# Softmax row sums of a pair of heads: one product on four column tiles, reciprocals spread by SBUF transfers

## The chip, the cores and the metric

The kernel runs on one core of a Trainium2 chip. The metric is the device time of one execution in microseconds (us), lower is better; the figure for a kernel is the median of several runs.

## What is computed

Two layers of a hybrid backbone over 1024 latent tokens and 256 context tokens, width 1024. Layer 0 mixes with a recurrence and a Fourier transform. Layer 1, where the change lies, is attention with 16 heads of 64 values, queries of 1024 tokens over keys and values of all 1280 tokens, followed by a gate, an output projection and a layer norm:

```python
def attend(q, k, v):
    s = jnp.einsum('bqhd,bkhd->bhqk', q, k, preferred_element_type=jnp.float32) * ATTN_SCALE
    p = jax.nn.softmax(s, axis=-1).astype(v.dtype)
    return jnp.einsum('bhqk,bkhd->bqhd', p, v)
...
    o_l = blocked_attention(q_l, k_all, v_all).reshape(b_, s_, MLA_WIDTH)
    y_lat = (o_l * jax.nn.silu(g_l)) @ w_out
```

All data are float32. A softmax needs, for each head and query, the sum of the exponentials over all 1280 keys, and its reciprocal.

## The kernel before

**Loops.** The attention stage walks over eight pairs of heads (`p`, 0 to 7); a pair over two halves of the queries (`hf`, 512 each); a half over ten key tiles of 128 keys (`kt`, called units here). The two heads of a pair, `a`, lie on two row groups of TensorE, so that their score products run side by side. `attend` issues a unit's ten score products into one of two score tiles in PSUM (`s`), the exponential on ScalarE into one of six tiles `p`, and on GpSimd the addition of `p` to the running sum `ra` (128 keys by 2 heads by 512 queries), one such addition per unit. `pv` multiplies the exponentials of a unit with the values into `st["o"]`, the one bank of the pool `o_ps`; units 3, 5, 7 and 9 run it for two earlier units, and the last two units (8 and 9) are left to `rest`, which runs in the next half.

**The ends of a half.** `finish` gives a table of what the next half (or the next pair's first half) runs after a given unit. `rest` (unit 1): the last two `pv`, then on VectorE the gate tile `sgt` times the result `po`. `rows` (unit 3): the row sums, two products of `ra` with a 128x64 tile of ones on two column tiles, so that each head's sums stand on 64 rows of PSUM, the same on each, and a ScalarE copy to `ri`. `piece` 0 to 3 (units 4 to 7): the reciprocals of `ri` on VectorE, 128 columns at a time. `last` (unit 8): on VectorE `sgt` times `ri`, both in SBUF, and the store to `o_dr`. A pair runs all of it twice.

**What runs between.** While pair `p` is attended, the next is prepared. `near` and `far` hold steps that are run after a unit's scores and at its end. In units 2 to 17 of a pair's twenty they are mostly `max_pass`, which finds the greatest score of each query for pair `p + 1`: per tile of 128 queries three steps (512, 512 and 256 keys), each with two heads. A step takes two tiles `mx` of the pool `m_ps` (line 827), which has three banks that go round, writes both with TensorE (line 977) and reduces each on VectorE (line 979). An even unit has one step of 512 keys, an odd unit one of 512 near and one of 256 far. Also in `far`: in even pairs the weights of the next four heads (`prep_quad`, with the loads of the rotary tables `rc` and `rs`), in odd pairs the values (`prep_v`, one more bank of `m_ps`). Units 18 and 19 have no steps of the pass but its end. In pairs 6 and 7 the output weights are loaded and split (`wo1_load`, `wo1_high`, `wo1_low`, lines 1033 to 1050): a load waits until GpSimd has split what was in its buffer.

**Order.** TensorE, VectorE, ScalarE and GpSimd run what is written, in that order (`manual_schedule`, line 998). All loads and stores of this stage are issued by SyncE, one queue, whose order is set when the program is built; an issue that waits holds back those behind it.

Of the kernel before, what the change touches and what calls it, by code (L numbers as in the profile page):

```python
# [13 lines left out]
F32 = mybir.dt.float32  # L14
F32R = mybir.dt.float32r
AF = mybir.ActivationFunctionType
ALU = mybir.AluOpType
# [4 lines left out]
P = 128  # L22
# [5 lines left out]
NT = T // P  # L28
# [26 lines left out]
def _body(ctx, tc, ap, out, dbg=None):  # L55
# [4 lines left out]
    def load(o, i):  # L60
        nc.sync.dma_start(out=o, in_=i)
# [801 lines left out]
    def prep_quad(q):  # L863
# [23 lines left out]
        def ra(hf):  # L887
            c = slice(512 * hf, 512 * hf + 512)

            def product():  # L890
                pa = m_ps.tile([P, 512], F32, tag="m", name=f"pra{q}{hf}")
                for k in range(2):
                    mm3(pa, wh[:, k, 2, :], wl[:, k, 2, :], qnh[k][:, c], qnl[k][:, c], k == 0, k == 1)
                rc = pr_p.tile([P, 512], F32, tag="rc", name=f"rc{q}{hf}")
                load(rc, ap["ropec_cm"][:, c])
                rs = pr_p.tile([P, 512], F32, tag="rs", name=f"rs{q}{hf}")
                load(rs, ap["ropes_cm"][:, c])
                rot = pr_p.tile([P, 512], F32, tag="rot", name=f"rot{q}{hf}")
                V.stream_shuffle(out=rot, in_=pa, mask=[i ^ 8 for i in range(32)])
                V.tensor_tensor(out=rc, in0=rc, in1=pa, op=ALU.mult)  # L900
                st[hf] = rc, rs, rot

            def turn():
                rc, rs, rot = st[hf]
                G.tensor_tensor(out=rot, in0=rot, in1=rs, op=ALU.mult)
                G.tensor_tensor(out=rot, in0=rot, in1=rc, op=ALU.add)

            def parts():
                split(roth[:, c], rotl[:, c], st[hf][2], S, G)

            return [product, turn, parts]
# [146 lines left out]
    def attend(p, hf, kt, st):  # L1058
# [2 lines left out]
        c = slice(512 * hf, 512 * hf + 512)  # L1061
        ks = slice(P * kt, P * kt + P)
        if kt == 0:
            st["sg"] = at.tile([P, 512], F32, tag="sgt", bufs=2, name=f"sgt{p}{hf}")
            load(st["sg"], sg_dr[p][:, c])
            st["o"] = o_ps.tile([P, 512], F32, tag="o", name=f"po{p}{hf}")
            st["ra"] = at.tile([P, 2, 512], F32, tag="ra", bufs=2, name=f"ra{p}{hf}")
            if p == 7:
                st["rv"] = at.tile([P, 2, 512], F32, tag="rv", name=f"rv{hf}")
            st["e"] = []  # L1070
        b = p % 2
        ps = s_ps.tile([P, 2, 512], F32, tag="s", name=f"s{p}{hf}{kt}")

# [17 lines left out]
    def pv(p, st, k):  # L1091
        q, i = divmod(p, 2)
        for a in range(2):
            TE.matmul(st["o"][64 * a : 64 * a + 64, :], quad[q][6][:, k, 128 * i + 64 * a : 128 * i + 64 * a + 64],  # L1094
                      st["e"][k][:, a, :], start=(k == 0), stop=(k == NT - 1), tile_position=(0, 64 * a))

    def finish(p, hf, st):

        c = slice(512 * hf, 512 * hf + 512)

        def rest():
            for k in (8, 9):
# [21 lines left out]
            load(o_dr[p][:, c], st["sg"])  # L1124

        if p == 7 and hf == 0:
            return {1: [rest], 2: [rows], 3: [piece(0), piece(1)], 4: [piece(2)], 5: [piece(3), last]}
        return {1: [rest], 3: [rows], 4: [piece(0)], 5: [piece(1)], 6: [piece(2)], 7: [piece(3)], 8: [last]}

    def o_load(t):  # L1130
# [16 lines left out]
    for p in range(8):  # L1147
# [37 lines left out]
        for hf in range(2):  # L1185
            st = {}
            for kt in range(NT):
                g = NT * hf + kt
                attend(p, hf, kt, st)
                for u in near[g]:  # L1190
                    u()
                if kt > 2 and kt % 2:
                    pv(p, st, kt - 3)
                    pv(p, st, kt - 2)
                for u in tail.get(kt, ()):
                    u()
                for u in far[g]:
                    u()
                if p == 7 and g == 18:
                    os_ = {0: o_load(0)}  # L1200
            tail = finish(p, hf, st)

    s_psc()
    f_ps, f_psc = pool("f_ps", 2, space=PSUM)
# [184 lines left out]
```

## Time and profile before

| what | value |
|---|---|
| median of three runs | 1445.64 us (1443.05 to 1446.84) |
| the profiled execution, its own time | 1445.85 us |
| its span, first to last instruction | 1444.0 us |
| TensorE busy | 1396.4 us (97%) |
| VectorE, GpSimd, ScalarE busy | 911.3, 678.7, 542.2 us |
| attention, from the first scores of pair 0 to the last of pair 7 | 838.1 to some 1340 us |

The profile is one execution on the chip. Times in its views are us from the span's start, PE is TensorE, DVE is VectorE, ACT is ScalarE, POOL is GpSimd, SPq is SyncE's queue. A float32 product shows as two matmul records. Matmul ends are modelled, so what a group of products costs is read from where the next one starts. A TensorE that waits in its queue can still look busy; the chain of waits and the starts tell it.

### The profile page before, as it was taken

To read this page: it belongs to the slowest core of one execution; us is meant where nothing else is said; L and a number is where in the kernel's file an instruction comes from. 1 tells how busy PE (TensorE), PEld (TensorE's weight loads), DVE (VectorE), ACT (ScalarE), POOL (GpSimd) and SP (SyncE) were. 2 spreads that over 40 slices of the span, in tenths; PEclk is the share of its full clock that TensorE was granted. 3 is DMA by queue.
4 is the path that set the end of the run, shared out by engine and by line. 5 is a ranking of instruction groups with operands and counts; after the bars stand their busy time and mean duration, and the time that the engine had idled before them with its cause. 6 is when DMAs were issued, how large, how long until landed. Compare 5 with 4: busy or idle time off the path is not lost.

```text
span 1444.0 us, 19804 instructions
## 1 busy us (share of the span) xinstructions
PE 1396.4 (97%) x7912; PEld 1019.3 (71%) x7912; DVE 911.3 (63%) x1454; ACT 542.2 (38%) x664; POOL 678.7 (47%) x314
## 2 busy tenths in 40 slices
PE   6998999999999999999999999999999999999997
PEld 3776777777888878887987765666565556554686
DVE  5659868665755443236844546658576757564798
ACT  2276666656112221103432143443434344445210
POOL 1124434444201233412232158767766876799643
PEclk9999999999999999999999999999999999999999
DMA  8713233233302474321043131111101010124432
GB/s 301 249 52 113 98 114 105 93 106 107 126 16 91 147 243 136 114 78 34 16 146 113 52 99 37 37 46 47 53 16 37 30 38 16 39 70 146 133 131 88
DMA packets 65869, 134.10 MB, mean 93 GB/s; under 512 B 5864, under 2 KB 31720, under 8 KB 63472
## 3 DMA queue, kind: packets, MB, share of 16 engines
q1 hardware_dynamic: 63328, 124.83, 27.0%
q0 software_dynamic: 2016, 7.60, 1.4%
q8 instruction: 62, 1.02, 0.3%
q10 hardware_dynamic: 432, 0.39, 0.1%
q14 instruction: 31, 0.25, 0.1%
HBM read 101.14 MB, written 24.66 MB: 87 GB/s over the span
## 4 chain that ended last, share of the span: by engine, by line
PE 74%; DVE 16%; DMA 3%; ACT 2%; issue 2%; POOL 1%; SPq 0%; DVEq 0%; POOLq 0%; ACTq 0%
PE s L1078 12%; PE z L267 11%; PE y L646 10%; PE po L1094 9%; PE mx L977 6%; PE yf L1212 5%; PE in1g L85 2%; PE in1g L87 2%; PE in1g L86 2%; DVE xc L317 2%; DVE gate L367 1%; DVE th L362 1%; DVE gate L378 1%; DVE m L979 1%; DMA woraw<-in_wo 1%
## 5 line engine op out<-in xcount | busy, mean ns | idle before, releaser
L1084 POOL TENSOR_TENSOR ra<-ra,p 128x1024 f32<-128x1024 f32 x112 | 269.8, 2409 | 99.3 <-ACT p L1080 95.3
L979 DVE TENSOR_REDUCE m<-mx 128x1 f32<-128x512 f32 (+1 forms) x384 | 209.4, 589 | 76.0 <-PE mx L977 75.1
L1080 ACT ACTIVATE p<-s 128x1024 f32<-128x1024 f32 x160 | 163.5, 1025 | 175.4 <-PE s L1078 171.9
L267 PE MATMUL z<-uh,w0h 128*128 128x512 f32 (+1 forms) x576 | 149.6, 366 | 4.4 <-ACT uh L76 4.4
L82 POOL TENSOR_TENSOR w0l<-w,w0h 128x1024 fp32r<-128x1024 f32 x24 | 64.0, 2666 | 184.7 <-DVE w0h L78 102.3
L267 PE MATMUL z<-ul,w0h 128*128 128x512 f32 (+1 forms) x576 | 147.7, 362 | 0.0
L267 PE MATMUL z<-uh,w0l 128*128 128x512 f32 (+1 forms) x576 | 147.5, 361 | 0.0
L267 PEld LDWEIGHTS z<-uh,w0h 128*128 128x128 f32 x576 | 98.2, 190 | 33.3 <-issue 11.5
L267 PEld LDWEIGHTS z<-ul,w0h 128*128 128x128 f32 x576 | 96.7, 190 | 18.7 <-issue 1.2
L267 PEld LDWEIGHTS z<-uh,w0l 128*128 128x128 f32 x576 | 96.3, 190 | 18.3 <-issue 2.0
L1078 PE MATMUL s<-R,KR 64*128 64x512 f32 (+1 forms) x640 | 104.9, 392 | 0.0
L345 ACT ACTIVATE gate<-gps,vec 128x512 f32<-128x512 f32 (+1 forms) x96 | 57.5, 616 | 103.3 <-PE gps L87 103.1
L977 PE MATMUL mx<-Kh,Qh 64*128 64x512 f32 (+1 forms) x384 | 86.4, 396 | 1.8 <-DVE m L979 1.5
L1094 PE MATMUL po<-p,v_even 128*64 128x512 f32 x320 | 77.5, 605 | 0.0
L1094 PE MATMUL po<-p,v_odd 128*64 128x512 f32 x320 | 77.5, 605 | 0.0
L977 PEld LDWEIGHTS mx<-Kh,Qh 64*128 64x128 f32 x384 | 43.0, 185 | 48.6 <-DVE m L979 26.8
L977 PE MATMUL mx<-KR,R 64*128 64x512 f32 (+1 forms) x384 | 77.1, 357 | 0.0
L381 POOL TENSOR_TENSOR gate<-gate,gate 128x1280 f32<-128x1280 f32 x8 | 23.9, 2990 | 112.3 <-DVE gate L378 97.1
L1078 PEld LDWEIGHTS s<-R,KR 64*128 64x128 f32 (+1 forms) x640 | 64.7, 184 | 12.3
L1078 PE MATMUL s<-Qh,Kh 64*128 64x512 f32 x320 | 70.6, 413 | 0.5 <-DVE sg L1024 0.5
L649 DVE TENSOR_TENSOR n<-gbc,y 128x1024 f32<-128x1024 f32 x10 | 12.2, 1222 | 87.3 <-PE y L646 87.3
L1078 PE MATMUL s<-Qh,Kl 64*128 64x512 f32 x320 | 67.3, 390 | 0.0
(358 smaller groups left out, 3091.2 us busy)
## 6 DMA issues: line engine op xcount, KB each, us to landing
w<-in_w SPq DMA_DIRECT2D x24, 512.0 KB
adaw<-in_ada SPq DMA_DIRECT2D x32, 256.0 KB
adawm<-in_ada SPq DMA_DIRECT2D x8, 1024.0 KB
adawg<-in_ada_g SPq DMA_DIRECT2D x8, 1024.0 KB
y_dr<-sg SPq DMA_DIRECT2D x10, 640.0 KB
woraw<-in_wo SPq DMA_DIRECT2D x12, 512.0 KB
xt<-in_x_cm SPq DMA_DIRECT2D x8, 640.0 KB
yra<-y_dr SPq DMA_DIRECT2D x10, 512.0 KB
```

The costliest lines, as they stand in the source:

```text
L82: el.tensor_tensor(out=lo, in0=src, in1=f(hi), op=ALU.subtract)
L85: TE.matmul(o, lh, rh, start=start, stop=False)
L267: TE.matmul(z[:, a : a + n], wi[:, kt, :], ui[kt][:, a : a + n], start=(kt == 0 and ui is uh and wi is wh), stop=(kt == KT - 1 and wi is wl))
L345: S.activation(out=gt[d, g][:, a : a + n], in_=ps[:, :n], func=AF.Sigmoid, bias=vv("gateb", 4 * j + i))
L646: TE.matmul(ps[:, 512 * hf : 512 * hf + 512], a[k], b[k][:, 512 * hf : 512 * hf + 512], start=(k == 0 and a is yh and b is woh), stop=(k = ...
L977: TE.matmul(ps[a][:, :n], q[r, P * t : P * t + P], k[r, a0 : a0 + n], start=st, stop=not st)
L979: V.tensor_reduce(out=m3s[t][:, a, i : i + 1], in_=ps[a][:, :n], axis=AX.X, op=ALU.max)
L1078: TE.matmul(ps[:, a, :], k[r, ks], w[r, c], start=(j == 0), stop=(j == len(parts) - 1))
L1080: S.activation(out=es, in_=ps, func=AF.Exp, scale=SCALE)
L1084: G.tensor_tensor(out=ra, in0=st["e"][0] if kt == 1 else ra, in1=es, op=ALU.add)
L1094: TE.matmul(st["o"][64 * a : 64 * a + 64, :], quad[q][6][:, k, 128 * i + 64 * a : 128 * i + 64 * a + 64], st["e"][k][:, a, :], start=(k == ...
L1212: TE.matmul(ps[i], a[:, k, :], b[k][:, pieces[i]], start=(k == 0 and a is oh and b is w1o), stop=(k == 7 and a is ol))
```

## The change

For pairs 0 to 6 the ends of both halves are gathered at the end of the pair. The first half leaves only `rest`, now after unit 2 of the second half instead of unit 1. After the second half, in the next pair's first half: `rest` (unit 1); one `rows` for both halves, four products on four column tiles of 32 columns, so that the four sums (two halves by two heads) stand on 32 rows each; one ScalarE copy; four pieces of reciprocals, the second and third both in unit 5; then `spread_rows`, which builds the 128-row tile `rb` of the first half's reciprocals with four SyncE transfers of 32 rows from SBUF to SBUF; `last(0)` in unit 8, the product for the first half, its store, and the transfers for the second half into the same `rb`; and `last(1)` in unit 11, which is unit 1 of the next pair's second half. The gate tile `sgt` is loaded in unit 9 instead of unit 0. `ra` has three buffers, and to make room `rc` and `rs` are loaded into the buffers of `wk` and `wq`, once those are split. Pair 7 keeps its own ends, with its first half's `rest` and `rows` both after unit 2.

```diff
@@ ra(hf).product in prep_quad @@
-                rc = pr_p.tile([P, 512], F32, tag="rc", name=f"rc{q}{hf}")
+                rc = pr_p.tile([P, 512], F32, tag="wk", name=f"rc{q}{hf}")
                 load(rc, ap["ropec_cm"][:, c])
-                rs = pr_p.tile([P, 512], F32, tag="rs", name=f"rs{q}{hf}")
+                rs = pr_p.tile([P, 2, 3, P], F32, tag="wq", name=f"rs{q}{hf}").rearrange("p a b c -> p (a b c)")[:, 0:512]
                 load(rs, ap["ropes_cm"][:, c])
@@ attend @@
         if kt == 0:
-            st["sg"] = at.tile([P, 512], F32, tag="sgt", bufs=2, name=f"sgt{p}{hf}")
-            load(st["sg"], sg_dr[p][:, c])
             st["o"] = o_ps.tile([P, 512], F32, tag="o", name=f"po{p}{hf}")
-            st["ra"] = at.tile([P, 2, 512], F32, tag="ra", bufs=2, name=f"ra{p}{hf}")
+            st["ra"] = at.tile([P, 2, 512], F32, tag="ra", bufs=3, name=f"ra{p}{hf}")
             if p == 7:
-                st["rv"] = at.tile([P, 2, 512], F32, tag="rv", name=f"rv{hf}")
+                st["rv"] = at.tile([P, 2, 512], F32, tag="ra", bufs=3, name=f"rv{hf}")
             st["e"] = []
+        if kt == 9:
+            st["sg"] = at.tile([P, 512], F32, tag="sgt", bufs=2, name=f"sgt{p}{hf}")
+            load(st["sg"], sg_dr[p][:, c])
@@ new: finish_pair(p, hf, st), which finish calls for p < 7 @@
+        if hf == 0:
+            pending[p] = st
+            return {2: [rest]}
+        sts = [pending.pop(p), st]
+
+        def rows():
+            rp = m_ps.tile([P, 512], F32, tag="m", name=f"rp{p}")
+            for i in range(4):
+                TE.matmul(rp[32 * i : 32 * i + 32, :], ones[:, 0:32], sts[i // 2]["ra"][:, i % 2, :], start=True, stop=True,
+                          tile_position=(0, 32 * i))
+            st["ri"] = at.tile([P, 512], F32, tag="ri", name=f"ri{p}")
+            S.copy(out=st["ri"], in_=rp)
...
+        def spread_rows(h):
+            def run():
+                st["rb"] = at.tile([P, 512], F32, tag="rb", name=f"rb{p}{h}")
+                for i in range(4):
+                    r = 64 * h + 32 * (i // 2)
+                    load(st["rb"][32 * i : 32 * i + 32, :], st["ri"][r : r + 32, :])
+            return run
+
+        def last(h):
+            def run():
+                sg = sts[h]["sg"]
+                V.tensor_tensor(out=sg, in0=st["rb"], in1=sg, op=ALU.mult)
+                load(o_dr[p][:, 512 * h : 512 * h + 512], sg)
+            return run
+
+        return {1: [rest], 3: [rows], 4: [piece(0)], 5: [piece(1), piece(2)], 6: [piece(3), spread_rows(0)],
+                8: [last(0), spread_rows(1)], 11: [last(1)]}
@@ finish, pair 7 @@
-            return {1: [rest], 2: [rows], 3: [piece(0), piece(1)], 4: [piece(2)], 5: [piece(3), last]}
+            return {2: [rest, rows], 3: [piece(0), piece(1)], 4: [piece(2)], 5: [piece(3), last]}
@@ the loop: what is left of a table goes on into the next half, ten units earlier @@
+            left = {k - NT: v for k, v in tail.items()}
             tail = finish(p, hf, st)
+            for k, v in left.items():
+                tail.setdefault(k, []).extend(v)
```

VectorE around unit 1 of pair 3's second half, before (`mx44..` are the score tiles of pair 4's query tile 4, by step and head):

```order
L979 TENSOR_REDUCE m344_8988<-mx4400_8989 128x1
L979 TENSOR_REDUCE m344_8988<-mx4401_8990 128x1
L979 TENSOR_REDUCE m344_8988<-mx4410_9011 128x1
L979 TENSOR_REDUCE m344_8988<-mx4411_9012 128x1
L1104 TENSOR_TENSOR sgt30_8626<-sgt30_8626,po30_8628 128x512
L979 TENSOR_REDUCE m344_8988<-mx4420_9032 128x1
```

The same stretch now:

```order
L979 TENSOR_REDUCE m344_8993<-mx4400_8994 128x1
L979 TENSOR_REDUCE m344_8993<-mx4401_8995 128x1
L979 TENSOR_REDUCE m344_8993<-mx4410_9016 128x1
L979 TENSOR_REDUCE m344_8993<-mx4411_9017 128x1
L1138 TENSOR_TENSOR sgt21_8600<-rb21_8928,sgt21_8600 128x512
L979 TENSOR_REDUCE m344_8993<-mx4420_9034 128x1
```

The product with `rb`, of pair 2's second half, has moved in between the second and the third step of the pass; the product with `po` has moved out, to after the next step.

TensorE in units 1 and 2 of pair 2's second half, before (`s212` are the scores of unit 2):

```order
L1094 MATMUL po20_7978<-p208_8269,v_odd_6673 64x512 x2
L1094 MATMUL po20_7978<-p209_8296,v_odd_6673 64x512 x2
L977 MATMUL mx3420_8375<-Kh1_6667,Qh1_6665 128x256
L977 MATMUL mx3421_8376<-Kh1_6667,Qh1_6665 128x256
L977 MATMUL mx3420_8375<-KR1_5764,R11_6669 128x256
L977 MATMUL mx3421_8376<-KR1_5764,R11_6669 128x256
L1078 MATMUL s212_8384<-Qh0_5773,Kh0_5775 128x512 x2
```

The same stretch now:

```order
L977 MATMUL mx3420_8374<-Kh1_6667,Qh1_6665 128x256
L977 MATMUL mx3421_8375<-Kh1_6667,Qh1_6665 128x256
L977 MATMUL mx3420_8374<-KR1_5764,R11_6669 128x256
L977 MATMUL mx3421_8375<-KR1_5764,R11_6669 128x256
L1079 MATMUL s212_8383<-Qh0_5773,Kh0_5775 128x512 x2
```

The four value products of `po20`, which stood between the two steps of unit 1, have gone to the end of unit 2, after the step `mx350.`.

SyncE's queue in pair 6's first half, before (`w1oraw` are output weights, `sgt` gate tiles, `R21` rotary rows for the next pair):

```order
L61 DMA R21_6670<-rotl3_9282 32x1024
L61 DMA w1oraw2_10813<-in_wo1 128x1024
L61 DMA o_dr_4920<-sgt51_10278 128x512
L61 DMA sgt61_10914<-sg_dr_4919 128x512
L61 DMA w1oraw3_10941<-in_wo1 128x1024
```

The same stretch now:

```order
L61 DMA R21_6670<-rotl3_9280 32x1024
L61 DMA w1oraw2_10823<-in_wo1 128x1024
L61 DMA rb50_10817<-ri5_10718 32x512 x4
L61 DMA o_dr_4920<-sgt50_10246 128x512
L61 DMA rb51_10885<-ri5_10718 32x512 x4
L61 DMA sgt60_10890<-sg_dr_4919 128x512
L61 DMA w1oraw3_10955<-in_wo1 128x1024
```

Eight transfers of reciprocals have come in; the first four stand behind the load of `w1oraw2`.

## Rows read from the trace of the kernel before

**Rows 1.** The page: busy time, share of the span and instructions of each engine.

```profile
PE 1396.4 (97%) x7912; PEld 1019.3 (71%) x7912; DVE 911.3 (63%) x1454; ACT 542.2 (38%) x664; POOL 678.7 (47%) x314
```

**Rows 2.** Busy time by stretch: pair 3's second half (PE, PEld, DVE, ACT, POOL; granted clock).

```profile
1070.90:1100.70 29.80, 29.80 (x210) 17.82 (x208) 19.29 (x38) 12.02 (x13) 19.49 (x9) 1.00 0.05 17
```

**Rows 3.** The chain that ended last, from 1000 us: start, us, what.

```profile
1001.63 2.12 DVE sgt L1123
...
1004.40 0.50 PE mx L977 x3
```

**Rows 4.** Timeline of TensorE, layer 0: a group on four column tiles (start, us).

```profile
62.48 1.06 PE L166 MATMUL adam<-adawm,cond 128*32 128x512 f32 x8
63.47 0.85 PE L267 MATMUL z<-uh,w0h 128*128 128x512 f32 x3
```

**Rows 5.** Timeline of TensorE, pair 3: row sums, then the second half.

```profile
1049.61 1.03 PE L1111 MATMUL rp<-ra,ones 128*64 128x512 f32 x4
1050.56 0.39 PE L977 MATMUL mx<-Kh,Qh 64*128 64x256 f32 x2
...
1070.87 0.51 PE L1078 MATMUL s<-Qh,Kh 64*128 64x512 f32 x2
...
1074.35 1.94 PE L1094 MATMUL po<-p,v_odd 128*64 128x512 f32 x8
1076.22 0.39 PE L85 MATMUL pv<-wkh,kvh 128*128 128x256 f32 x1
...
1079.11 0.39 PE L1078 MATMUL s<-Qh,Kh 64*128 64x512 f32 x2
```

**Rows 6.** Timeline of VectorE, pair 2's end: `last` in unit 18.

```profile
1031.67 0.67 DVE L1123 TENSOR_TENSOR sgt<-ri,sgt 128x512 f32<-128x512 f32 x1
```

**Rows 7.** Timeline of VectorE, pair 3, units 8 and 11.

```profile
1066.90 2.48 DVE L1123 TENSOR_TENSOR sgt<-ri,sgt 128x512 f32<-128x512 f32 x1
...
1074.34 1.29 DVE L979 TENSOR_REDUCE m<-mx 128x1 f32<-128x512 f32 x2 [0.34 <-PE mx L977]
```

**Rows 8.** Timeline of GpSimd, the same stretch.

```profile
1066.46 5.16 POOL L1084 TENSOR_TENSOR ra<-ra,p 128x1024 f32<-128x1024 f32 x2 [1.63 <-ACT p L1080]
1075.15 2.37 POOL L1084 TENSOR_TENSOR ra<-p,p 128x1024 f32<-128x1024 f32 x1 [3.53 <-ACT p L1080]
```

**Rows 9.** Timeline of VectorE, pair 2, units 4 to 11.

```profile
990.06 0.94 DVE L1119 RECIPROCAL ri<-ri 128x128 f32<-128x128 f32 x1
...
991.67 0.74 DVE L979 TENSOR_REDUCE m<-mx 128x1 f32<-128x256 f32 x2
...
1008.06 1.29 DVE L979 TENSOR_REDUCE m<-mx 128x1 f32<-128x512 f32 x2 [0.33 <-PE mx L977]
```

**Rows 10.** Timeline of TensorE, pair 2, unit 6.

```profile
991.97 0.66 PE L977 MATMUL mx<-Kh,Qh 64*128 64x512 f32 x2
```

**Rows 11.** Timeline of TensorE, pair 2's second half, unit 3.

```profile
1011.91 0.40 PE L1078 MATMUL s<-Qh,Kh 64*128 64x512 f32 x2
```

**Rows 12.** Timeline of GpSimd, pair 2, unit 11.

```profile
1009.78 2.38 POOL L1084 TENSOR_TENSOR ra<-p,p 128x1024 f32<-128x1024 f32 x1
```

**Rows 13.** Timeline of SyncE's queue, pair 2: a load that waited for GpSimd.

```profile
1004.90 0.33 SPq L61 DMA_DIRECT2D rs<-in_ropes_cm  x1
```

**Rows 14.** Timeline of SyncE's queue, pair 6.

```profile
1232.03 1.20 SPq L61 DMA_DIRECT2D R<-roth  x2
...
1262.05 0.34 SPq L61 DMA_DIRECT2D w1oraw<-in_wo  x1
1264.95 0.33 SPq L61 DMA_DIRECT2D o_dr<-sgt  x1
1266.97 0.32 SPq L61 DMA_DIRECT2D sgt<-sg_dr  x1
```

**Rows 15.** Timeline of GpSimd, pair 6, units 7 to 9.

```profile
1261.99 7.64 POOL L1084 TENSOR_TENSOR ra<-ra,p 128x1024 f32<-128x1024 f32 x3
```

**Rows 16.** Timeline of TensorE, pair 6, unit 9: the step of 256 keys.

```profile
1265.46 0.50 PE L977 MATMUL mx<-Kh,Qh 64*128 64x256 f32 x2
```

More of the change, by code (lines that the diff above doesn't have):

```diff
@@ L1063, in attend @@
         if kt == 0:
+            st["o"] = o_ps.tile([P, 512], F32, tag="o", name=f"po{p}{hf}")
+            st["ra"] = at.tile([P, 2, 512], F32, tag="ra", bufs=3, name=f"ra{p}{hf}")
+            if p == 7:
+                st["rv"] = at.tile([P, 2, 512], F32, tag="ra", bufs=3, name=f"rv{hf}")
+            st["e"] = []
+        if kt == 9:
             st["sg"] = at.tile([P, 512], F32, tag="sgt", bufs=2, name=f"sgt{p}{hf}")
             load(st["sg"], sg_dr[p][:, c])
-            st["o"] = o_ps.tile([P, 512], F32, tag="o", name=f"po{p}{hf}")
-            st["ra"] = at.tile([P, 2, 512], F32, tag="ra", bufs=2, name=f"ra{p}{hf}")
-            if p == 7:
-                st["rv"] = at.tile([P, 2, 512], F32, tag="rv", name=f"rv{hf}")
-            st["e"] = []
         b = p % 2
@@ L1095, in pv, with finish_pair, rest, piece @@
                       st["e"][k][:, a, :], start=(k == 0), stop=(k == NT - 1), tile_position=(0, 64 * a))
+    pending = {}
+    def finish_pair(p, hf, st):
+        def rest():
+            for k in (8, 9):
+                pv(p, st, k)
+            V.tensor_tensor(out=st["sg"], in0=st["sg"], in1=st["o"], op=ALU.mult)
+        if hf == 0:
[9 more added lines that the diff above has]
+            S.copy(out=st["ri"], in_=rp)
+        def piece(b):
+            def run():
+                d = slice(P * b, P * b + P)
+                V.reciprocal(out=st["ri"][:, d], in_=st["ri"][:, d])
+            return run
[7 more added lines that the diff above has]
+        def last(h):
+            def run():
+                sg = sts[h]["sg"]
+                V.tensor_tensor(out=sg, in0=st["rb"], in1=sg, op=ALU.mult)
+                load(o_dr[p][:, 512 * h : 512 * h + 512], sg)
+            return run
+        return {1: [rest], 3: [rows], 4: [piece(0)], 5: [piece(1), piece(2)], 6: [piece(3), spread_rows(0)],
+                8: [last(0), spread_rows(1)], 11: [last(1)]}
     def finish(p, hf, st):
         c = slice(512 * hf, 512 * hf + 512)
+        if p < 7:
+            return finish_pair(p, hf, st)
         def rest():
@@ L1194, in _body @@
                     pv(p, st, kt - 2)
-                for u in tail.get(kt, ()):
+                for u in tail.pop(kt, ()):
                     u()
```

## The prediction

> **What bounds the kernel now.** The page first: TensorE is busy 97% of the span, VectorE 63% [rows 1]. Then the attention stage, by stretch: in pair 3's second half TensorE is busy for all of its 29.8 us at the full granted clock, VectorE for 19.3 and GpSimd for 19.5 [rows 2]. So in this stage a TensorE instruction taken away is time won, and work of another engine costs nothing until TensorE waits for it. The third view, the chain that ended last, shows where it does: at 1001.63 the product `last` of VectorE stands on it with 2.12 us, and behind it a reduction and TensorE's next maxima [rows 3]. The way is this: `mx` has three banks, a step takes two, so each step needs a bank of the step before, and that one is free only when VectorE has reduced it. Whatever VectorE does between two steps' reductions delays TensorE once the slack between the steps is used up.
>
> The length of `last` is not its own. In pair 2's unit 18 it takes 0.67 us [rows 6]; in pair 3's unit 8 it takes 2.48, from 1066.90 to 1069.38 [rows 7]. GpSimd's addition had begun at 1066.46, just before, and of two in 5.16 us the first, at the 2.37 that one takes, ended near 1068.83 [rows 8]: the product ended 0.55 later. Both inputs of `last` lie in SBUF; it seems to wait until the addition under way is over. The sixteen products in this kernel take 0.67 to 2.94 us. The eight of the first halves stand in unit 18, where no step of the pass follows, and most of those take 0.67.
>
> **The row sums.** Two products (four records) hold TensorE from 1049.61 to 1050.56, 0.95 us [rows 5]. The same shape as the new group, four products on four column tiles of 32 columns by 512, stands in layer 0: eight records, and the next product starts 0.99 us after the first [rows 4]. Pairs 0 to 6 give up 14 groups of 0.95 = 13.3 and take 7 of 0.99 = 6.9: **-6.4 us**. Bounds: -6.7 if the new group takes no longer than an old one, and 0 if four tiles took turns by two. The Trainium skill (TensorEngine Tiling (Array Packing), Key Properties) says that a change of the tiling mode drains TensorE; the group's 0.99 among products of full width holds whatever drain there was, and by a further drain that no row prices, the sum would be higher.
>
> **Reciprocals and copies.** 28 pieces of 0.94 [rows 9] and 7 copies leave VectorE and ScalarE. In the second halves of odd pairs TensorE does not wait for them, so nothing comes of that; in even pairs, where `prep_quad` loads VectorE too, it is at least nothing and at most one piece, 0.94, for each of three pairs (0 to -2.8). I take 0.2 each, **-0.6**, near the lower end, because what delays the reductions there, `prep_quad`'s own products on VectorE, stays.
>
> **The first halves** keep their four pieces, but two of them now stand in unit 5. In even pairs VectorE is without a gap there: the reduction of unit 5's third step starts at 991.67, its first bank is free at 992.04, and TensorE's step in unit 6, at 991.97, already waits for it [rows 9, 10]. One piece more ahead of it is 0.94 later, so 0.9 us in pairs 2 and 4 (pair 0 has no predecessor, pair 6 no `prep_quad`): **+1.8** (bounds 0 and 2.5).
>
> **Unit 11**, the main term. Two things meet in units 0 to 2 of every second half. The four value products of `rest`, 1.87 us from 1074.35 to 1076.22 [rows 5], leave unit 1, where they stood between the second and the third step and gave VectorE time; they come after unit 2's step. And `last(1)`, which stood in unit 8 of a half, comes between the reductions of the second and third step. Pair 3, in the times of before: VectorE ends the second step's reductions at 1074.34 + 1.29 = 1075.63 [rows 7]. `last(1)` is next, and GpSimd has begun an addition at 1075.15 that ends at 1077.52 [rows 8], so the product ends at 1078.07. The first bank of the third step is reduced at 1078.45 (half of 0.76). Unit 2's step waits for that bank; 0.5 us later it is through, then 1.87 for the value products: unit 3 begins at 1080.8 instead of 1079.11 [rows 5], **+1.7**, three odd pairs. Even pairs have no `prep_v` to fill unit 1. Pair 2: reductions end at 1008.06 + 1.29 = 1009.35 [rows 9]; with the odd pair's 2.44 from there to the product's end, 1011.8; +0.38 +0.5 +1.87 = 1014.5 against 1011.91 [rows 11], **+2.6**, pairs 2, 4 and 6. Pair 0 has no `last(1)`, but its third step follows its second without a pause and needs a bank that is free at 1008.06 + 0.65 = 1008.7 by pair 2's times, where TensorE comes at 1007.9: **+0.8**. Sum 0.8 + 5.1 + 7.8 = **+13.7**. From below: a product of 0.67 gives 0 in odd and 0.9 in even pairs, 3.5 in all. From above: the product comes just after an addition has begun, which for pair 2 is 1009.78 + 2.38 + 0.55 = 1012.7 [rows 12], +3.5, and +2.2 in an odd pair: 17.9. I take the phase that the rows show. Behind the product are queued only this pass's reductions and the product with `po`; for them TensorE waits, and no one else.
>
> **The transfers.** Each `spread_rows` is four issues of some 0.6 us (two transfers of 32 rows took 1.20 [rows 14]); a 256 KB store issued at 1264.95 had landed when the load behind it was issued at 1266.97, so I take 2.0 us to land [rows 14]. That is 1.8 + 2.0 = 3.8 us from the first issue to the last landing. In odd pairs nothing on SyncE waits ahead of them, and two units lie between the last piece and `last(0)`: hidden. In even pairs the second four stand behind the load of `rs`, which waited for GpSimd until 1004.90 [rows 13]: with an issue and a store ahead of them they land at 1009.5, about when `last(1)` wants them. The loads of `rc` and `rs`, now behind the splits of `wk` and `wq` in units 4 and 5, are used in unit 7: I take them as hidden; if not, VectorE waits there for at most a landing, 2.0, in each of three even pairs, which is in rival 1. In pair 6 it does not fit: the four stand behind `w1oraw2`, which waits for GpSimd until 1262.05 [rows 14]. First issue 1262.4, last landing 1266.2; GpSimd's second addition of that row ends at 1267.1 [rows 15], the product 0.55 later, the first reduction of unit 9 at 1268.3; TensorE wanted that bank at 1265.46 [rows 16]. **+2.8** (2.1 without the wait for GpSimd, at most 3.5). Pair 7 has no pass, and what it waits I take as hidden (at most 2).
>
> **The sum**: -6.4 - 0.6 + 1.8 + 13.7 + 2.8 = +11.3 on the profiled execution's 1445.85 (span 1444.0), 0.2 above the median: 1457. The lower bounds together are -6.7 - 2.8 + 0 + 3.5 + 2.1 = -3.9, the upper ones 0 + 0 + 2.5 + 17.9 + 3.5 + 2 = +26; not all ends meet, and with the four tiles side by side as the row shows it is about +20.
>
> **The rivals.** (1) Slower by more: phases against it, transfers late in even pairs as well. 1463 to 1468. For: GpSimd is the fuller engine in even pairs. Against: each delay of TensorE lets GpSimd catch up. (2) About the same: `last(1)` is not caught. It needs VectorE to come first; then GpSimd waits and the product takes 0.67, as in unit 18. With 3.5 for unit 11 and 2.1 for pair 6 the sum is -6.4 - 0.6 + 1.8 + 3.5 + 2.1 = +0.4, 1446. It decides by half a microsecond, 1075.15 against 1075.63. The Trainium skill (SBUF — State Buffer, Who interferes with whom) says that the two engines share a port pair under an exclusive lock, held by whichever starts first for the whole instruction; the 0.67 and the 2.48 agree with both outcomes. (3) Faster: the saved products are all that shows, because the delays of one step are made up in the next. That asks for slack on TensorE in the second halves, and rows 2 show none; 1445.6 - 6.4 = 1439. (4) The change does not do what it says: four tiles take as long as two and two, no saving, 1463.
>
> **How the numbers follow.** My forecast, 1457 within 4 us, 0.58; rival 1 0.12; rival 2 0.17; rival 3 0.08; rival 4 0.05. A difference of 0.3%, 4.3 us, is about what a measurement of this kernel can tell from no change, so 1441.3 and 1450.0 part the three outcomes. Faster: rival 3 and a sliver of rival 2, 0.09. Same: most of rival 2 and the near edge of the forecast, 0.16. Slower: 0.75. The range takes in the forecast, rivals 2 and 4 and most of rival 1: 1443 to 1467.
>
> **What would show it.** In the changed profile: a group of eight records `rp` in unit 3 of first halves, next product about 1 us on (step 1); the product with `rb` in unit 11 taking 2 us or more, unit 2's maxima and unit 3's scores late by 1.7 and 2.6 us (unit 11); second halves of odd pairs at about 30.6 us instead of 29.8 (+1.7 - 0.95), of even pairs at about 31.5; in pair 6 the product with `rb` starting after 1266 by the old clock. If those halves are shorter than 29.8, the term of unit 11 is wrong; if the product takes 0.67 there, rival 2 holds.

## The result: slower by 2.2%, and where the time went

The changed kernel takes 1477.67 us (median of 4 runs), the kernel before 1446.24 beside it: a ratio of 1.0223, 95% interval 1.0207 to 1.0238. The direction was forecast, the size was not: 31.4 us more instead of 11.3, and 10.7 beyond the upper end of the range. The profiled execution took 1478.94, its span 1477.2; its row of busy times answers to [rows 1]:

```profile
PE 1403.9 (95%) x7912; PEld 1018.4 (69%) x7912; DVE 905.4 (61%) x1426; ACT 538.5 (36%) x657; POOL 678.4 (46%) x314
```

VectorE and ScalarE lost the instructions that the change takes away, and TensorE, with as many as before, is busy for longer. The next rows are the busy times by stretch, from the first scores of pair 0 to those of pair 7's second half: length, then busy us of PE, PEld (TensorE's weight loads), DVE, ACT and POOL, then the granted clock as a share of full speed. First the kernel before, then the changed one.

```profile
838.10:1316.60 478.50, 473.68 (x3103) 282.08 (x3102) 311.10 (x548) 204.22 (x236) 360.42 (x161) 1.00 0.17 49
```

```profile
836.80:1347.90 511.10, 485.61 (x3102) 286.17 (x3100) 303.93 (x519) 200.17 (x229) 359.84 (x161) 0.98 0.18 53
```

This stretch is 32.6 us longer (the spans differ by 33.2). TensorE's idle time in it went from 4.8 us to 25.5, and its busy time from 473.7 to 485.6: the same products took longer. So there are two losses, waits and a lower clock. The same view by halves of a pair (pair 2's two halves, pair 3's second, pair 4's second, pair 6's two) shows where they lie:

```profile
968.60:1008.70 40.10, 37.44 (x224) 22.21 (x224) 28.17 (x42) 14.70 (x18) 26.34 (x13) 0.96 0.16 39
1008.70:1043.20 34.50, 31.38 (x198) 17.89 (x196) 20.16 (x38) 11.18 (x12) 25.94 (x15) 0.95 0.25 74
...
1079.60:1110.60 31.00, 29.96 (x206) 17.95 (x204) 18.23 (x34) 11.43 (x12) 19.54 (x9) 1.00 0.13 38
...
1150.80:1186.50 35.70, 32.57 (x198) 18.37 (x197) 18.52 (x38) 11.21 (x12) 25.98 (x15) 0.90 0.18 54
...
1253.80:1291.90 38.10, 33.67 (x220) 20.05 (x220) 21.45 (x36) 15.33 (x18) 27.98 (x13) 1.00 0.18 43
1291.90:1324.90 33.00, 30.76 (x194) 18.03 (x192) 18.37 (x35) 12.12 (x12) 21.29 (x10) 0.90 0.23 70
```

Before, these took 36.2, 30.0, 29.8, 30.0, 32.9 and 27.9 us, from one half's first scores to the next's, all at full clock. The odd pair is 1.1 longer, about as forecast (30.6 was said, 30.9 came by the starts of the scores). Pairs 2, 4 and 6 are 4 to 6 us longer in each half, and all that ran below full clock lies in them. An estimate of what that cost, with pair 4's first half (40.2 us at 0.96): 0.04 x 40.1 + 0.05 x 34.5 + 0.04 x 40.2 + 0.10 x 35.7 + 0.10 x 33.0 = 11.8 us.

The waits by their releaser (engine and line, what it waited for, us in total, times, longest), kernel before and changed kernel:

```profile
PEld mx L977 <- DVE m L979: 26.1, 43, 1.3
...
PE mx L977 <- DVE m L979: 1.5, 4, 0.9
```

```profile
PEld mx L977 <- DVE m L979: 48.5, 54, 4.3
PE mx L977 <- DVE m L979: 22.2, 17, 4.1
...
DVE sgt L1138 <- DMA rb<-ri: 8.5, 4, 4.0
```

TensorE's maxima wait for VectorE's reductions, in few and long waits, and VectorE four times for the new transfers (in pairs 2, 4, 6 and 7). Four places make most of it.

**Odd pairs, units 1 and 2 of the second half** (pair 3; GpSimd, VectorE, TensorE by time):

```profile
1083.92 2.38 POOL L1085 TENSOR_TENSOR ra<-p,p 128x1024 f32<-128x1024 f32 x1 [3.54 <-ACT p L1081]
```

```profile
1084.32 2.54 DVE L1138 TENSOR_TENSOR sgt<-rb,sgt 128x512 f32<-128x512 f32 x1
1086.78 0.74 DVE L979 TENSOR_REDUCE m<-mx 128x1 f32<-128x256 f32 x2
```

```profile
1087.25 0.50 PE L977 MATMUL mx<-Kh,Qh 64*128 64x512 f32 x1 [1.00 <-DVE m L979]
...
1089.78 0.51 PE L1079 MATMUL s<-Qh,Kh 64*128 64x512 f32 x2
```

The addition begins 0.4 us before the product, the product ends 0.56 behind it, the reduction comes after it, and TensorE waits 1.00 us. Units 1 and 2 take 8.50 us instead of 6.60: +1.9 (+1.7 was forecast).

**Pairs 2 and 4, unit 5 of the first half** (pair 2 is shown). The same product of VectorE, the scaling of `wk`, in the kernel before and in the changed one, and GpSimd's addition there:

```profile
990.92 0.83 DVE L882 TENSOR_SCALAR wk<-wk,vec 128x512 f32<-128x512 f32 x1
```

```profile
990.21 1.75 DVE L1124 RECIPROCAL ri<-ri 128x128 f32<-128x128 f32 x2
991.88 2.47 DVE L882 TENSOR_SCALAR wk<-wk,vec 128x512 f32<-128x512 f32 x1
994.27 0.74 DVE L979 TENSOR_REDUCE m<-mx 128x1 f32<-128x256 f32 x2
```

```profile
991.70 2.37 POOL L1085 TENSOR_TENSOR ra<-ra,p 128x1024 f32<-128x1024 f32 x1
```

The second reciprocal of unit 5 pushes the scaling 0.96 us back (0.80 counted from the half's first scores), to 0.18 us behind the start of the addition. Then TensorE, and busy times and clock (0.57) of the stretch behind its wait:

```profile
994.74 0.79 PE L977 MATMUL mx<-Kh,Qh 64*128 64x512 f32 x1 [2.24 <-DVE m L979]
```

```profile
994.74:998.50 3.76, 3.76 (x18) 2.71 (x18) 2.70 (x6) 1.50 (x3) 3.42 (x2) 0.57 0.26 69
```

0.57 is a mean: for most of this stretch the granted clock is at the lower of its two levels (1.2 and 2.4 GHz). A pair of score products starts every 0.43 us there and every 0.23 at full clock. Units 6 and 7 take 11.4 us instead of 7.4: +4 in each of pairs 2 and 4, where +0.9 was forecast.

**Pairs 2 and 4, unit 2 of the second half** (pair 2 first): SP's queue, then VectorE, GpSimd and TensorE.

```profile
1008.98 0.33 SPq L61 DMA_DIRECT2D rs<-in_ropes_cm  x1
1009.41 0.38 SPq L61 DMA_DIRECT2D o_dr<-sgt  x1
1009.95 2.44 SPq L61 DMA_DIRECT2D rb<-ri  x4
```

```profile
1013.86 2.92 DVE L1138 TENSOR_TENSOR sgt<-rb,sgt 128x512 f32<-128x512 f32 x1 [0.42 <-DMA rb<-ri]
```

```profile
1013.88 2.35 POOL L1085 TENSOR_TENSOR ra<-p,p 128x1024 f32<-128x1024 f32 x1
```

```profile
1017.17 0.50 PE L977 MATMUL mx<-Kh,Qh 64*128 64x512 f32 x1 [2.48 <-DVE m L979]
...
1017.83 3.08 PE L1095 MATMUL po<-p,v_odd 128*64 128x512 f32 x8
```

The transfers wait behind the load of `rs`, which waits for GpSimd. Their result comes 0.4 us late, as an addition begins (within 0.02 us by the profile): the worst phase. TensorE waits 2.48 us, and the eight value products behind that take 3.08 instead of 1.94, at the lower clock. In pair 4 the same four transfers, issued from 1152.04, come later, and the wait for them is itself the larger part:

```profile
1157.56 1.30 DVE L1138 TENSOR_TENSOR sgt<-rb,sgt 128x512 f32<-128x512 f32 x1 [2.05 <-DMA rb<-ri]
```

**Pair 6**: SP's queue, VectorE, TensorE.

```profile
1283.12 0.34 SPq L61 DMA_DIRECT2D w1oraw<-in_wo  x1
1283.55 2.41 SPq L61 DMA_DIRECT2D rb<-ri  x4
```

```profile
1288.93 1.93 DVE L1138 TENSOR_TENSOR sgt<-rb,sgt 128x512 f32<-128x512 f32 x1 [3.96 <-DMA rb<-ri]
```

```profile
1291.52 0.58 PE L977 MATMUL mx<-Kh,Qh 64*128 64x256 f32 x1 [4.08 <-DVE m L979]
```

From the first issue to the use it is 5.4 us (3.8 was taken), with a load of 512 KB just ahead in the queue; in pair 4, where a load and a store of 256 KB stand ahead as in pair 2, it is 5.5, in pair 2 3.9. What makes the difference was not tried. TensorE waits 4.08, and the clock falls again.

### The profile page after: what moved, and what is told of

Its sections match the earlier page's. It is cut to its first block, busy times and chain, and to the rows that moved or that the text cites. A ratio compares the mean times of both kernels' runs of the same rounds, so it can differ in the third digit from the quotient of the medians.

```text
span 1477.2 us, 19861 instructions
## 1 busy us (share of the span) xinstructions
PE 1403.9 (95%) x7912; PEld 1018.4 (69%) x7912; DVE 905.4 (61%) x1426; ACT 538.5 (36%) x657; POOL 678.4 (46%) x314
## 4 chain that ended last, share of the span: by engine, by line
PE 67%; DVE 20%; DMA 4%; issue 4%; ACT 3%; POOL 1%; SPq 1%; DVEq 0%; POOLq 0%; ACTq 0%
PE z L267 11%; PE s L1079 11%; PE y L646 10%; PE po L1095 9%; PE mx L977 6%; PE in1g L85 2%; DVE sgt L1138 2%; PE in1g L86 2%; PE in1g L87 2%; DVE m L979 2%; DVE xc L317 2%; PE yf L1267 1%; DVE gate L367 1%; DVE gate L378 1%; DMA woraw<-in_wo 1%
## 5 line engine op out<-in xcount | busy, mean ns | idle before, releaser
L267 PEld LDWEIGHTS z<-uh,w0h 128*128 128x128 f32 x576 | 98.0, 190 | 33.2 <-issue 11.5
L977 PE MATMUL mx<-Kh,Qh 64*128 64x512 f32 (+1 forms) x384 | 94.8, 403 | 22.5 <-DVE m L979 22.2
L267 PEld LDWEIGHTS z<-uh,w0l 128*128 128x128 f32 x576 | 96.0, 189 | 18.2 <-issue 2.0
L977 PEld LDWEIGHTS mx<-Kh,Qh 64*128 64x128 f32 x384 | 47.0, 188 | 71.3 <-DVE m L979 49.2
L977 PE MATMUL mx<-KR,R 64*128 64x512 f32 (+1 forms) x384 | 83.5, 367 | 0.0
L1079 PE MATMUL s<-Qh,Kh 64*128 64x512 f32 x320 | 73.8, 425 | 0.5 <-DVE sg L1024 0.5
L1079 PE MATMUL s<-Ql,Kh 64*128 64x512 f32 x320 | 69.3, 396 | 0.0
```

The costliest lines, as they stand in the source:

```text
L267: TE.matmul(z[:, a : a + n], wi[:, kt, :], ui[kt][:, a : a + n], start=(kt == 0 and ui is uh and wi is wh), stop=(kt == KT - 1 and wi is wl))
L977: TE.matmul(ps[a][:, :n], q[r, P * t : P * t + P], k[r, a0 : a0 + n], start=st, stop=not st)
L1079: TE.matmul(ps[:, a, :], k[r, ks], w[r, c], start=(j == 0), stop=(j == len(parts) - 1))
```

## The experiments

The table gives the time (median), its ratio to the kernel before run beside it, and the length of pairs 0 to 6 in the profile (first scores of pair 0 to first scores of pair 7) and of pair 7's first half.

| kernel | us | ratio, 95% interval | pairs 0-6 | pair 7, first half |
|---|---|---|---|---|
| before | 1446.24 | | 455.6 | 22.9 |
| changed | 1477.67 | 1.0223, 1.0207-1.0238 | 488.0 | 23.1 |
| `rest` in unit 1 | 1467.11 | 1.0147, 1.0132-1.0162 | 476.2 | 23.1 |
| last product late | 1466.45 | 1.0145, 1.0129-1.0161 | 469.8 | 29.7 |
| pieces 1, 1, 2 | 1471.59 | 1.0163, 1.0135-1.0191 | 481.8 | 23.0 |
| no transfers | 1460.30 | 1.0098, 1.0082-1.0113 | 469.1 | 23.1 |
| SP's order | 1467.34 | 1.0153, 1.0133-1.0174 | 476.5 | 26.7 |
| wait filled | 1474.55 | 1.0204, 1.0189-1.0219 | 481.3 | 23.1 |
| three repairs | 1450.95 | 1.0042, 1.0025-1.0059 | 464.5 | 26.8 |
| and last product late | 1449.89 | 1.0035, 1.0021-1.0049 | 455.4 | 26.9 |
| and two loads moved | 1442.78 | 0.9985, 0.9977-0.9994 | 450.8 | 23.1 |
| and pair 7's `rest` | 1441.08 | 0.9968, 0.9956-0.9979 | 450.4 | 23.1 |
| changed, no additions | 1445.36 | 1.0001, 0.9991-1.0010 | 453.4 | 23.2 |
| before, no additions | 1439.90 | 0.9960, 0.9945-0.9976 | 450.0 | 23.0 |

**`rest` in unit 1.**

```diff
-            return {2: [rest]}
+            return {1: [rest]}
```

> The changed kernel with the first half's `rest` (last two products of po, multiplication by the gate) back in unit 1 of the second half; all else as changed. Theory A (VectorE gives the maxima's PSUM banks back too late, because the last multiplication, lengthened beside GpSimd's additions, lies between two steps' reductions; every such wait of TensorE that is long enough also brings stretches at the lower clock): the move of `rest` is no cause, the multiplication still stands in unit 1, so 1474 to 1481 us, and the second halves keep their 1.0 to 5.9 us. Rival B (the move of `rest` into unit 2, where it meets two max steps, is what costs): about 1 us per pair comes back, 1468 to 1471 us.

It came out at 1467.1, 10.6 us faster: theory A was wrong on this point, and rival B, with 1468 to 1471, nearly right. Units 1 and 2 of odd pairs take 6.60 us, as before the change, though `last(1)` still stands in unit 1. VectorE there, pair 3:

```profile
1080.38 0.69 DVE L1106 TENSOR_TENSOR sgt<-sgt,po 128x512 f32<-128x512 f32 x1 [0.71 <-PE po L1095]
1080.98 1.13 DVE L1138 TENSOR_TENSOR sgt<-rb,sgt 128x512 f32<-128x512 f32 x1
1082.04 0.74 DVE L979 TENSOR_REDUCE m<-mx 128x1 f32<-128x256 f32 x2
```

With the value products back in unit 1, VectorE waits for them first, meets the addition near its end (1.13 instead of 2.54 us), and TensorE has 1.9 us of value products more to do ahead of the third step. So in odd pairs neither move costs alone what both cost together. Pairs 2 and 4 keep a loss: their units 1 and 2 still take 7.7 and 10.5 us, 5.7 before the change.

**The last product late.**

```diff
-                8: [last(0), spread_rows(1)], 11: [last(1)]}
+                8: [last(0), spread_rows(1)], 18 if p < 6 else 11: [last(1)]}
```

> The changed kernel with the second half's last multiplication seven units later, in unit 8 of the next pair's second half, where no max step stands (pair 6's stays at unit 11, in pair 7). Transfers, products and reciprocals as changed. Theory A: the second halves of pairs 1 to 6 go back to their lengths before in units 1 and 2 (1.0 us in pair 0's neighbour, 1.9 in each odd pair, 4.9 and 5.9 in pairs 2 and 4, about 5 in pair 6, with the clock's stretches behind them), 1452 to 1457 us; the first halves of pairs 2 and 4 keep their 4 us and pair 6's unit 9 its 4.5. Rival C (the transfers themselves, on SP's queue and beside the other loads, hold the work up, wherever their result is used): under 8 us come back, 1469 us or more.

1466.5, between the two. Pairs 0 to 6 got 18.2 us shorter, somewhat less than theory A's 21 to 26: units 1 and 2 of odd pairs take 7.10, so `rest` in unit 2 costs half a microsecond by itself. And 6.6 us went to a new wait in pair 7, which neither theory had: SP issued the load of pair 6's second `sgt` behind a load of `w1oraw` that waits for GpSimd.

```profile
1310.33 0.33 SPq L61 DMA_DIRECT2D w1oraw<-in_wo  x1
...
1311.23 0.38 SPq L61 DMA_DIRECT2D sgt<-sg_dr  x1
```

```profile
1317.73 3.68 PE L1095 MATMUL po<-p,v_odd 128*64 128x512 f32 x8 [4.32 <-DVE sgt L1106]
```

**Reciprocals 1, 1, 2 over units 4 to 6.**

```diff
-        4: [piece(0)], 5: [piece(1), piece(2)], 6: [piece(3), spread_rows(0)],
+        4: [piece(0)], 5: [piece(1)], 6: [piece(2), piece(3), spread_rows(0)],
```

> The changed kernel with one reciprocal in unit 5 and two in unit 6, instead of two and one. Theory A with the collision at the weights (the second reciprocal of unit 5 pushes the scaling of wk into GpSimd's addition, 0.83 to 2.47 us, TensorE waits 2.2 us and then runs 3.4 us at the lower clock): the first halves of pairs 2 and 4 lose 3 to 4 us each, units 6 and 7 together go from 11.4 to about 8, and the kernel takes 1469 to 1472 us. Rival D (two reciprocals in one unit cost the same wherever they stand): 1476 to 1479 us.

As theory A said: 1471.6 (one of the four runs took 1464.7), and the scaling of `wk` takes 0.96 us, not 2.47; units 6 and 7 of pairs 2 and 4 take 7.56. Two reciprocals in unit 6 cost 0.15, two in unit 5 cost 4: it is what they push, not that there are two.

```profile
990.12 0.96 DVE L882 TENSOR_SCALAR wk<-wk,vec 128x512 f32<-128x512 f32 x1
```

**Without the transfers.**

```diff
-                st["rb"] = at.tile([P, 512], F32, tag="rb", name=f"rb{p}{h}")
-                for i in range(4):
-                    r = 64 * h + 32 * (i // 2)
-                    load(st["rb"][32 * i : 32 * i + 32, :], st["ri"][r : r + 32, :])
+                st["rb"] = st["ri"]
```

> The changed kernel without the SBUF transfers of the reciprocals: the last multiplications read ri as it is (left out: the spread of the reciprocals over the rows). Theory A: the odd pairs keep their 1.9 us, pair 0's neighbour its 1.0 and the first halves of pairs 2 and 4 their 4; what goes is the late landing in the even pairs (2 to 3 us each with its share of the clock) and pair 6's wait of 4 us in unit 9: 1462 to 1467 us. Rival C (the transfers are the cause of nearly all): 1446 to 1452 us. Rival E (the transfers cost nothing): 1476 us or more.

1460.3: 17.4 us came back, 1.7 more than theory A's most. Odd pairs keep their 1.9, the first halves of pairs 2 and 4 theirs (3.9 and 2.4); unit 2 of the even second halves falls from 7.7 and 8.8 us to 4.3, pair 6's unit 9 from 8.4 to 3.9. Of the parts of the change the transfers cost most, but not by their length in odd pairs, where nothing waits for them.

The two first halves differ in the clock alone: units 6 and 7 of pair 4 take 9.86 us, pair 2's 11.30. In pair 4 TensorE waits as long as in the changed kernel, and this time the clock does not fall:

```profile
1132.40 0.50 PE L977 MATMUL mx<-Kh,Qh 64*128 64x512 f32 x1 [2.20 <-DVE m L979]
```

```profile
1130.00:1137.00 7.00, 4.80 (x28) 2.54 (x28) 6.12 (x9) 2.57 (x3) 5.90 (x4) 1.00 0.25 75
```

So some 1.6 of the 17.4 us are not the transfers' doing. The same wait of pair 4 left the clock at full in the runs with the last product late and with SP's order. In the attention of all the traces fifteen waits of TensorE were 2.1 to 2.3 us long; a lower clock followed eleven of them and not the other four. What decides is not shown here.

**SP's queue in the order of the program.**

```diff
-    order.enter_context(tc.manual_schedule(engines={e.engine for e in (TE, V, S, G)}))
+    order.enter_context(tc.manual_schedule(engines={e.engine for e in (TE, V, S, G, nc.sync)}))
```

> The changed kernel with SP's DMA issues in the order in which the program writes them, from the attention's preparation on: the transfers rb<-ri then stand ahead of the load of rs in pairs 2 and 4 and ahead of the third load of w1oraw in pair 6, which wait for GpSimd. Theory F (of what leaving the transfers out gave, 17.4 us, most is their place behind loads that wait for GpSimd, not their own length): unit 2 of the second halves of pairs 2 and 4 goes from 7.7 and 8.8 us to about 4.3, unit 9 of pair 6 from 8.4 to about 4, the kernel takes 1459 to 1465 us. Rival C (the transfers' own length, four issues of 0.6 us and about 2 us of flight, is what comes too late): 1471 us or more.

Theory F holds for pair 2 (unit 2: 4.27) and pair 6 (unit 9: 3.94). It failed in pair 4: the transfers now go ahead of the load of `rc`, VectorE waits for that, and in the second half unit 2 takes 7.8 us though no transfer is late (its product takes 2.44 us, as in odd pairs; TensorE waits 1.50, and the granted clock is 0.67 from 1152 to 1162, while pair 2's product takes 1.12 and its clock stays full). Pair 7's first half is 3.6 us longer, by the wait described under the last product. So the sum, 1467.3, misses the forecast.

```profile
1141.44 0.69 DVE L900 TENSOR_TENSOR rc<-rc,pra 128x512 f32<-128x512 f32 x1 [2.02 <-DMA rc<-in_ropec_cm]
```

**The wait filled with work**, to see whether the clock is a cause of its own.

```diff
+                if p in (3, 5) and (t, i) in ((2, 0), (5, 0)):
+                    for _ in range(8):
+                        TE.matmul(ps[0][:, :n], Qh[b][0:64, P * t : P * t + P], Kh[b][0:64, a0 : a0 + n], start=True, stop=True)
```

> The changed kernel with eight more products of TensorE (about 1.9 us, their result is overwritten) in front of each of the four max steps of pairs 2 and 4 at which it waits 2.2 to 2.9 us for a bank (units 6 of the first and 2 of the second half); the wait is filled, nothing else is moved. Theory G (a long wait of TensorE brings the fall of the granted clock to 0.5, which costs 1.7 to 3.4 us behind the wait): the granted clock stays at 1.0 behind those four steps and the kernel gets faster by added work, by 5 to 8 us, 1470 to 1473 us. Rival H (the fall belongs to something else in these places, or the products delay what the wait hid): 1477 us or more, the clock falls as before.

TensorE in pair 2's unit 2 and the stretch's busy times and clock:

```profile
1014.28 2.00 PE L976 MATMUL mx<-Kh,Qh 64*128 64x512 f32 x8
1016.12 0.39 PE L980 MATMUL mx<-Kh,Qh 64*128 64x512 f32 x1
1017.22 0.49 PE L980 MATMUL mx<-Kh,Qh 64*128 64x512 f32 x1 [0.72 <-DVE m L982]
...
1017.87 1.94 PE L1098 MATMUL po<-p,v_odd 128*64 128x512 f32 x8
```

```profile
1016.00:1020.00 4.00, 3.28 (x16) 1.12 (x16) 3.09 (x7) 0.00 (x0) 2.98 (x2) 1.00 0.22 72
```

The third product starts at 1017.22, where it started at 1017.17 without the eight: the wait was only filled. The clock stays at 1.00, and the value products take 1.94 instead of 3.08. The same at the other three places: pairs 2 to 4 take 210.6 us instead of 217.9. On the clock theory G holds. The kernel as a whole, 1474.55, stayed above the forecast, and its gain on the changed kernel is not clear of noise (the intervals of the two ratios overlap). The attention is 6.8 us shorter, but 2.9 of it are lost ahead of and behind it in the profiled run (3.9 in all, 3.1 between the medians).

**Three repairs** (`rest`, pieces and SP's order as above), and the last product late with them.

> The changed kernel with three repairs: `rest` of the first half in unit 1 again, one reciprocal in unit 5 and two in unit 6, SP's issues in the order of the program. If the three causes add up (10.6 us, 6 us and about 14 us came back or would come back one at a time): 1445 to 1450 us, no stretch at the lower clock in the attention; what then remains is the gain on the row sums (7 times 0.6 us) against 1 to 2 us of pair 7 and the end. If they overlap or a new wait appears: 1452 us or more.

> As the kernel with the three repairs, and the second half's last multiplication in unit 8 of the next pair's second half instead of unit 1 (pair 6's unchanged). If the multiplication is covered by the products of `rest` in unit 1 in every pair: within 2 us of the other. If the even pairs still wait for it there: 3 to 6 us faster than the other.

1450.95 and 1449.89. The causes nearly add up; 27 of 31 us are back. The rest lies in three places: VectorE waits 2.2 us for `rc` in pairs 2 and 4 (the fault of SP's new order), and pair 7 waits as above. With the product late, pairs 0 to 6 are 9 us shorter in the profile, more than the 1 us between the medians of the two; the first kernel's profiled run, 1457.7, is the highest of its nine, so its profile overstates its waits.

**Two loads moved**: `rc` and `rs` of pairs 2 and 4 ahead of the transfers (`early` holds the two loads of `ra(0)`, taken out of its `product`), the sixth `w1oraw` behind pair 6's `sgt`.

```diff
+                near[6].append(early[p // 2 + 1, 0])
...
-        if k + 2 < 8:
+        if k + 2 < 8 and k != 3:
             wo1_load(k + 2)
...
+            if p == 7:
+                near[1].append(lambda: wo1_load(5))
```

> As the kernel with three repairs and the last multiplication in unit 8, and SP's queue repaired at the two places where that kernel still waits: the first loads of rc and rs of pairs 2 and 4 stand ahead of the transfers (VectorE waited 2.2 us for rc), and the sixth load of w1oraw stands behind the load of pair 6's second sgt (TensorE waited for that in unit 3 of pair 7, 7.7 instead of 4.0 us). If the remaining 9 us in these three places are SP's order alone: 1440 to 1443 us, no stretch at the lower clock in the attention, faster than the kernel before by 0.1 to 0.3%. If something else waits there: 1446 us or more.

1442.8, as expected: no stretch of the attention is below full clock, and pairs 0 to 6 are 4.8 us shorter than before the change.

**Pair 7's `rest` back.**

```diff
-            return {2: [rest, rows], 3: [piece(0), piece(1)], 4: [piece(2)], 5: [piece(3), last]}
+            return {1: [rest], 2: [rows], 3: [piece(0), piece(1)], 4: [piece(2)], 5: [piece(3), last]}
```

> As the kernel with all repairs so far, and pair 7's first half's `rest` and row sums in units 1 and 2 of its second half, as before the change, instead of both in unit 2. Units 1 to 3 there take 11.1 us in that kernel, 9.8 in the changed one and 9.6 before. If the place of `rest` is the reason: 1 to 1.5 us faster than that kernel, 1441 to 1442 us. If not: no difference within 0.6 us.

1441.1, 5.2 us faster than the kernel before: it beats both. Against the kernel ahead of it the gain is doubtful: units 1 to 3 take 10.65 us, 0.45 less instead of 1 to 1.5, and the intervals of the two ratios touch. Its row for the stretch shown first, and pair 3's second half, which answers to [rows 2]:

```profile
836.20:1309.70 473.50, 468.87 (x3103) 279.77 (x3102) 290.82 (x519) 200.19 (x229) 360.45 (x161) 1.00 0.19 57
```

```profile
1066.80:1095.70 28.90, 28.90 (x204) 17.52 (x202) 16.46 (x34) 11.44 (x12) 19.47 (x9) 1.00 0.09 26
```

TensorE is idle for 4.6 us, as before, and busy for 4.8 less: that is about what the merged row sums are worth.

**Without GpSimd's additions**, changed kernel and kernel before.

```diff
-            if p < 7 or kt == 1:
+            if p < 7:
+                if kt == 1:
+                    G.memset(ra, 1.0)
+            elif kt == 1:
                 G.tensor_tensor(out=ra, in0=st["e"][0] if kt == 1 else ra, in1=es, op=ALU.add)
```

> The changed kernel without GpSimd's additions for the row sums in pairs 0 to 6 (left out: the sums over the key tiles; a constant stands in their place). Theory A in its form that GpSimd's additions make VectorE's products with two operands in SBUF long: last takes 0.7 instead of 2.5 us, the scaling of wk 0.8, unit 2 of the odd pairs' second halves goes from 5.1 to about 3.7 and units 6 and 7 of pairs 2 and 4 to about 8 together; the loads that wait for GpSimd come earlier too: 1446 to 1454 us. Rival I (the products' place in VectorE's order is enough, whatever their length): 1465 us or more.

> The kernel before without GpSimd's additions for the row sums in pairs 0 to 6 (left out: the sums over the key tiles; a constant stands in their place). The changed kernel without them took 1445.4 us, 32 less than with them. If GpSimd's hold on the long products is what the change ran into, the kernel before must lose little by it: 1438 to 1443 us, so that without the additions the two differ by 2 to 7 us, not 31. If the additions cost the kernel before as much (whatever delays there are), it falls to 1425 us or less and the change costs as much as with them.

1445.4, 0.6 below theory A's range, and 1439.9, within its own. Without the additions the change costs 5.5 us, with them 31.4 (3.3 and 32.4 in pairs 0 to 6); the kernel before gains 6 by their absence. The group of the new last product over pairs 0 to 6 (busy us, mean ns of one), changed kernel and the same without additions:

```profile
L1138 DVE TENSOR_TENSOR sgt<-rb,sgt 128x512 f32<-128x512 f32 x14 | 31.8, 2270 | 8.5 <-DMA rb<-ri 8.5
```

```profile
L1141 DVE TENSOR_TENSOR sgt<-rb,sgt 128x512 f32<-128x512 f32 x14 | 11.7, 838 | 2.2 <-DMA rb<-ri 2.2
```

So 26 of the 31 us need GpSimd at work. This run alone doesn't part two ways in which it acts, the long products and the loads that wait for it on SP. Without the transfers, where no product waits for a late landing, some 14 of the 31 us are left.

## Why the prediction fell short, step by step

The forecast was 20 us too low. The step that failed most is the price of a wait: each was put at its own length, and the lower clock behind it stood in no term. The step on the first halves failed as well, by its mechanism; the others were right in kind, with their sizes off.

- **Row sums, -6.4.** Right in kind, too large. The four-tile group takes 0.99 us, as forecast. What comes back is 5.1 us over pairs 0 to 6 in the best kernel (450.4 against 455.6): 0.73 us a pair, not 0.9. In the changed kernel unit 3 of second halves got 0.74 shorter (5.70 to 4.96) and unit 3 of first halves 0.14 longer.
- **Unit 11, odd pairs +1.7 and pair 0 +0.8.** Right: 1.9 and 0.9, by the mechanism and the phase that were given. That the two moves must meet was in the working (the value products "gave VectorE time"), and the run with `rest` in unit 1 shows it.
- **Unit 11, even pairs +2.6 each.** Too small: 4.9 and 6.0 in units 1 and 2 of pairs 2 and 4, 4.4 in pair 6. I gave the product the odd pair's phase. In pair 2 the transfers landed where the working had them (4.1 us later by a half that began 4.1 later), but that made the product wait until an addition began, which was the upper bound (+3.5). In pair 4 they landed 1.9 us later than that, which the working did not allow for in this term. The clock came on top in all three pairs.
- **First halves, +1.8.** This step failed: 8.0 us in units 6 and 7 of pairs 2 and 4, some 4.8 of them without the lower clock. I priced the extra reciprocal as a shift of 0.94 and let the next product, the scaling of `wk`, keep its 0.83 us. I had applied GpSimd's hold to `last` alone, because it has two operands in SBUF. The Trainium skill (SBUF — State Buffer, Who interferes with whom) names `tensor_scalar` as well among the instructions that can take the ports shared with GpSimd; 0.83 us beside 2.47 agrees.
- **Pair 6, +2.8.** Mechanism right, size off: 4.5 us in unit 9 and 1.4 in the unit behind it. The landing was 1.6 later than taken, and a lower clock followed the wait.
- **The clock**: not in the sum at all, and the largest miss, some 11.8 us. [rows 2] shows full clock, and TensorE's longest wait for a reduction in the attention of the kernel before was 1.3 us. I forecast waits of up to 3 us and priced each at its own length. The Trainium skill (TensorE: Matmul & The Clock Gate, Part 1: The HAM clock gate) says that the array falls to half its clock when it has been idle; the row at 0.57 behind a wait of 2.24 us agrees. The 1.00 us waits of odd pairs left the clock at 1.00, and so did four of the fifteen waits of 2.1 to 2.3 us: the term could have been bounded, hardly forecast.

The terms at their upper ends, with the saving, made "about +20"; with the 11.8 of the clock that is 32, and 31.4 was measured. That these meet is partly luck. Less their shares of the 11.8, unit 11 and pair 6 cost some 19 us together, below their bounds' 21.4, and the first halves 4.8, above their 2.5. Rival 1 named the mechanism (phases against it, late transfers), at 17 to 22 us. The late first halves are not what made the second ones late: with pieces 1, 1, 2 the first halves are on time and unit 2 of the even second halves still takes 8.8 us.

One thing stays open: behind the attention the changed kernel is some 1.7 us longer, and the variants too, though nothing is changed there. VectorE's last products stand later against TensorE's last; what shifts them was not tried. The kernel before without its additions shows 1.3 us of it, so it is not the change alone.

## What to carry to other kernels

Price a wait of TensorE, where it bounds the kernel, at its length, and give the sum an upper bound with what the lower clock can cost behind it (here an estimated 3.6 us in pair 4's second half, 0.10 of its 35.7); look first at the longest one. When an instruction is pushed back, look at the next ones on its engine, too: each may come to stand beside another engine's instruction that holds it up, as the scaling of `wk` did, and its old duration is then void. A transfer is hidden only if nothing ahead of it in its queue waits: read the queue's issue times, not the transfer's length; the idea was worth 5 us once the queue, the reciprocals and the two moved products were in order.

## What the runs showed of the hardware

Adding 32 products made a kernel no slower, and its attention 6.8 us shorter, because TensorE did not fall idle and its clock stayed at full. Waits of much the same length (2.1 to 2.3 us) were followed by half clock eleven times and not four times. An SBUF transfer of four parts of 32 rows took 2.4 us of issue, and 3.9, 5.4 and 5.5 us from the first issue to the use at three places where VectorE waited for it. VectorE's product of two SBUF tiles took 1.13 us when an addition of GpSimd was near its end, 2.54 when one had begun 0.4 us earlier and 2.92 when one began with it.
